# Pairs of heads put two to a step for the y and the p.v products, and 64 columns of ones in the sums over features

## The chip, the cores and the metric

The kernel runs on one core of a Trainium2 chip. The metric is the device time of one execution in microseconds (us); the median of three runs before the change is 1227.45 us (1226.97 to 1230.41). The core has five engines that run side by side: TensorE (PE in the rows, its weight loads PEld), VectorE (DVE), ScalarE (ACT), GpSimd (POOL), and SyncE (SP), which issues the loads. Matrix products are written to PSUM banks and taken out of them by VectorE and ScalarE.

## The reference

Two layers, each a mixer and a feed-forward net, on 256 tokens of 1024 features in float32. The mixer runs sparse attention and a state-space scan side by side; the lines below are those that the change touches.

```python
for l in range(DEPTH):                                   # DEPTH = 2
    h = rms_norm(x, norm1_g[l]) * (1.0 + sc1) + sh1
    proj = h @ w_in[l]                                   # 1024 x 10856
    ...
    s = jnp.einsum("bqhd,bqkhd->bhqk", qb, kg) * scale   # 16 heads of 64
    p = jax.nn.softmax(s, axis=-1)
    o = jnp.einsum("bhqk,bqkhd->bqhd", p, vg)            # the p.v products
    o_attn = o @ w_attn_o[l]
    ...
    cb = jnp.einsum("bclgn,bcsgn->bgcls", cm_c, bm_c)    # 4 groups of 8 heads
    y_diag = jnp.einsum("bgcls,bgrcls,bcsgrp->bclgrp", cb, decay, xs_c)   # the y products
    y = rms_norm((y + xs * d_skip) * silu(z), by group)  # a sum of squares over features
    o_ssm = y @ w_ssm_o[l]
    mixed = (sigmoid(ga) * o_attn + sigmoid(gm) * o_ssm) @ w_out[l]
    x = x + g1 * mixed
    h = rms_norm(x, norm2_g[l]) * (1.0 + sc2) + sh2      # a sum of squares over features
    u = causal_dwconv(h @ w_up[l])
    x = x + g2 * ((silu(gate) * val) @ w_down[l])
```

## The kernel before

Everything is kept with features on the partitions and the 256 tokens along the free dimension. Each float32 weight and activation is split into a high and a low part that TensorE takes at one pass (ScalarE copies the high part, `wh` for weights; VectorE subtracts it, `wl`), and each product of 128 x 128 weights with 256 tokens is three instructions: hi.hi, hi.lo, lo.hi. These are the main products, 8112 of them (`bk<-h,wh`, `bk<-u,wl` and the like), run by `run_fm` and `run_tm` in one fixed order, the chunks of `plan`. After every 12 of them (one output tile of a unit of 4 weight tiles) comes a call of `pump()`, which may let one step of side work into TensorE's program.

Side work is written as generators. `attention` (line 1582) and `ssd` (line 1688) stand in the queue `calm`, of which only the first is advanced, one step in a call. A step ends with `yield Need(...)`: the next one is let in when the tiles named are due by the kernel's own reckoning of time, and when as many of the four small PSUM banks as `banks=` says are free. So the place of each step among the main products follows from a planner's reckoning (`on_pe`, `after`, `plan_ahead`), and so does the order of instructions on VectorE, ScalarE and GpSimd, where each waiting piece has a priority (`urgent` raises it).

Two heads make a pair. For each of 8 pairs in a layer, `attention` does scores and softmax in step n, six transposes in step n+2 (`pT`), and the p.v products in step n+3 (lines 1626 to 1640): four float32 products with 64-column weights, 256 and 128 tokens wide for either head, then `hi_lo` of the result. For each of 16 pairs in a layer, `ssd` makes the decay in step n (a product with `sel`, ScalarE's `Exp`, VectorE's product with `cbm`) and the y products in step n+2 (lines 1719 to 1731): again four products with 64-column weights, then one VectorE instruction that adds `x_[i]` times `dsk`. A float32 product is two instructions in the trace, so one block of a pair is eight.

`token_sum` (line 1196) sums squares over features: two float32 products in which a 128 x 128 tile of squares is the weights and 16 columns of `ones` are moved; `inv_rms` reads one column of each.

```python
# lines 1201 and 1215
mm(st["ps"][:, 16 * t:16 * t + 16], sq[:, t * P:t * P + P], ones[:, 0:16], ...)
total = st["ps"][:, 0:32].rearrange("p (t c) -> p t c", c=16)[:, :, 0]
```

The adaLN weights of later layers are summed on VectorE in the gaps (`adacc`) and folded by TensorE (`bk<-adacc,ones`, weights of 32 columns). All instructions are issued by one helper, so every row of the profile has line 209, and rows are told apart by tile names: `p` is the shared tile of `pe`, `pT` and the decay `e`; `u` holds v, x, z and the split parts.

Of the kernel before, what the change touches and what calls it, by code (L numbers as in the profile page):

```python
# [15 lines left out]
ALU = mybir.AluOpType  # L16
# [3 lines left out]
P = 128  # L20
# [26 lines left out]
def trunk(ctx, tc, x, c, positions, w_ada, b_ada, norm1_g, w_in, q_norm_g, k_norm_g, ssm_conv_w, ssm_conv_b,  # L47
# [197 lines left out]
    def done(*tiles):  # L245
        for t in tiles:
            held.discard(t.tensor.name)
# [240 lines left out]
    def bank(pool=None):  # L488
        cnt[0] += 1
        pool = pool or sm  # L490
        t = pool.tile([P, 512], F32, tag="bank", name=f"bk{cnt[0]}")
        if pool is sm:
            bank_tag[0] = t.tensor.tag
        return t

    def mm(o, lhsT, rhs, start, stop):
        return T.matmul(o, lhsT, rhs, start=start, stop=stop, skip_group_check=True)
# [698 lines left out]
    def token_sum(st, total, sq):  # L1196
        def task():
            if st["ps"] is None:
                st["ps"] = bank()
            for t in range(2):  # L1200
                mm(st["ps"][:, 16 * t:16 * t + 16], sq[:, t * P:t * P + P], ones[:, 0:16],
                   st["n"] == 0 and t == 0, st["n"] == total - 1)
            st["n"] += 1
            if st["n"] == total and "then" in st:
                st["then"]()
            yield

        first_of_all.append(later(Need(sq, banks=0 if st["n"] else 1), task()))

    def inv_rms(st, scale, eps):  # L1210

        v = w_tile("rv", [P, 2])
        total = st.get("sum")
        if total is None:
            total = st["ps"][:, 0:32].rearrange("p (t c) -> p t c", c=16)[:, :, 0]
        st["rv"] = V.tensor_scalar(v, total, scale, eps, op0=ALU.mult, op1=ALU.add)
        r = w_tile("rr2", [P, 2])
        G.tensor_tensor(r, v, mhalf, op=ALU.pow)
        return r
# [117 lines left out]
    def mixer(l, link, link_out):  # L1337
# [244 lines left out]
        def attention(heads):  # L1582
# [4 lines left out]
            for n in range(len(pairs) + TD + PD):  # L1587
                if n < len(pairs):
# [20 lines left out]
                    with urgent():  # L1609
                        V.reciprocal(sums, sums)  # L1610
                        for j in range(2):
                            for t, cs in HALF:
                                G.tensor_scalar(pe[:, j, cs], pe[:, j, cs], sums[:, j, t:t + 1], 0.0, op0=ALU.mult, op1=ALU.add)
                if n - TD in pes:
                    pe = pes.pop(n - TD)
                    yield Need(pe, banks=2)
                    pT = pTs[n - TD] = hold(w_tile("pT", [P, 2, 384]))
                    pts = [bank(), bank()]
                    for j in range(2):
                        for b in range(3):  # L1620
                            T.transpose(pts[j][:, b * P:b * P + P], pe[:, j, b * P:b * P + P], ident)
                    done(pe)
                    with urgent():
                        for j in range(2):
                            A.activation(pT[:, j], pts[j][:, 0:384], AF.Copy)
                if n - TD - PD in pTs:
                    pT = pTs.pop(n - TD - PD)
                    i = pairs[n - TD - PD]
                    yield Need(pT, *vt[0][i // 4], *vt[1][i // 4], banks=1)
                    po = bank()  # L1630
                    for t, cs, src in ((0, slice(0, S), slice(0, S)), (1, slice(P, S), slice(S, 384))):
                        for j in range(2):
                            hh = 2 * i + j
                            vs = slice((hh % 4) * 64, (hh % 4) * 64 + 64)
                            mm(po[64 * j:64 * j + 64, cs], vt[t][hh // 8][(hh % 8) // 4][:, vs], pT[:, j, src], t == 0, t == 1)
                    done(pT)
                    if i % 2 == 1:
                        done(*(vt[t][i // 4][(i % 4) // 2] for t in range(2)))
                    with urgent():
                        hi_lo(po[:, 0:S], oT, i)  # L1640


        def ev_conv(base, dst, then=None):
# [44 lines left out]
        def ssd(g):  # L1688
# [12 lines left out]
            for n in range(4 + 2):  # L1701
                if n < 4:
# [13 lines left out]
                    yield Need(e, on="dve")  # L1716
                    with urgent():
                        V.tensor_tensor(e, e, cbm[g][:, None, :].to_broadcast([P, 2, 384]), op=ALU.mult)
                if n >= 2:
                    i = n - 2  # L1720
                    e = es.pop(i)
                    yield Need(e, cbm[g], *xdt, banks=1)
                    py = bank()
                    for cs, x, src in ((slice(0, S), xdt[0], slice(0, S)), (slice(P, S), xdt[1], slice(S, 384))):
                        for j in range(2):
                            hs = slice((2 * i + j) * 64, (2 * i + j) * 64 + 64)
                            mm(py[64 * j:64 * j + 64, cs], x[:, hs], e[:, j, src], x is xdt[0], x is xdt[1])
                    done(e)
                    m = 4 * g + i
                    with urgent():  # L1730
                        V.scalar_tensor_tensor(x_[i], x_[i], dsk[:, l, m:m + 1], py[:, 0:S], op0=ALU.mult, op1=ALU.add)
            while None in z_:
                yield
            warm.append(ssd_norm(g))
# [203 lines left out]
```

## Time and profile before

| | us |
|---|---|
| median of 3 runs | 1227.45 |
| lowest, highest | 1226.97, 1230.41 |
| the profiled execution | 1227.39 |
| its span from first to last instruction | 1225.7 |
| TensorE busy in it | 1201.3 (98%) |
| VectorE busy | 991.4 (81%) |
| ScalarE busy | 775.3 (63%) |
| GpSimd busy | 494.1 (40%) |

A matmul's row has a modelled end: it is told as 0.28 us long where the next one starts 0.11 to 0.12 us later. So a busy TensorE is read by the steps from start to start, and a row's idle time is 0.17 us less than what a wait costs.

### The profile page before, as it was taken

The page shows a single profiled execution, that of the slowest core. Times are in us where ns is not written, and L with a number is a line of the kernel's source. Part 1 is how long each engine was busy: PE and PEld are TensorE (multiplying, and loading weights), DVE is VectorE, ACT ScalarE, POOL GpSimd, SP SyncE. Part 2 cuts the span into 40 slices and gives each one's busy share as a digit, 9 for nine tenths or more (in the row PEclk, how much of TensorE's full clock was granted, in tenths as well). Part 3 has the DMA queues.
Part 4 walks back from the last instruction along what each step waited for, and adds up shares of the span by engine and source line. Part 5 has one row for each costly group of instructions (what it writes and reads, how often), then busy time and mean ns, then how long its engine had stood idle before and what let it go on. Part 6 is the DMA issues. An engine that isn't in the chain of part 4 may idle for free.

```text
span 1225.7 us, 24837 instructions
## 1 busy us (share of the span) xinstructions
PE 1201.3 (98%) x9835; PEld 1118.9 (91%) x9835; DVE 991.4 (81%) x1549; ACT 775.3 (63%) x1397; POOL 494.1 (40%) x503
## 2 busy tenths in 40 slices
PE   8999999999999999999999999999999999999998
PEld 7777898899988999999998778899999999999998
DVE  5488998778988789989767899888778757988863
ACT  4365577767865468778535557878578535877742
POOL 2163442216445225766202356314605313457710
PEclk9999999999999999999999999999999999999999
DMA  9765656655557666777665566264664665667551
GB/s 307 241 208 178 200 180 212 207 193 195 190 181 241 232 198 198 240 240 260 206 229 186 204 206 199 87 215 134 216 218 156 211 220 189 190 198 232 179 205 64
DMA packets 158665, 246.55 MB, mean 201 GB/s; under 512 B 11868, under 2 KB 66870, under 8 KB 158549
## 3 DMA queue, kind: packets, MB, share of 16 engines
q1 hardware_dynamic: 157989, 244.77, 60.1%
q8 instruction: 77, 1.26, 0.4%
q14 instruction: 39, 0.32, 0.1%
q0 software_dynamic: 288, 0.19, 0.1%
q10 hardware_dynamic: 272, 0.00, 0.0%
HBM read 243.89 MB, written 1.05 MB: 200 GB/s over the span
## 4 chain that ended last, share of the span: by engine, by line
PE 81%; DVE 12%; ACT 2%; issue 2%; POOL 1%; DMA 1%; SPq 0%; DVEq 0%; POOLq 0%; ACTq 0%
PE bk L209 81%; DVE wl L209 5%; DVE w L209 2%; DVE adacc L209 1%; ACT wh L209 1%; DVE p L209 1%; DVE u L209 1%; DVE t L209 1%; ACT w L209 1%; POOL rr L209 0%; DMA ad<-in_w_ada_dram 0%; POOL rows L209 0%; DVE top L209 0%; DVE mx L209 0%; POOL w L209 0%
## 5 line engine op out<-in xcount | busy, mean ns | idle before, releaser
L209 PE MATMUL bk<-h,wh 128*128 128x256 f32 x3296 | 588.1, 281 | 1.2 <-ACT h L209 1.1
L209 PEld LDWEIGHTS bk<-h,wh 128*128 128x128 f32 x3296 | 500.9, 189 | 12.0 <-issue 8.2
L209 DVE TENSOR_TENSOR wl<-st,wh 128x2048 fp32r<-128x2048 f32 (+1 forms) x200 | 439.8, 2206 | 67.3 <-ACT wh L209 67.0
L209 PE MATMUL bk<-h,wl 128*128 128x256 f32 x1648 | 457.9, 278 | 1.7 <-DVE wl L209 1.7
L209 ACT ACTIVATE wh<-st 128x2048 fp32r<-128x2048 f32 (+1 forms) x200 | 352.8, 1770 | 154.8 <-PE bk L209 129.9
L209 POOL TENSOR_TENSOR w<-w,w 128x254 f32<-128x254 f32 (+2 forms) x213 | 254.9, 1209 | 252.7 <-DVE w L209 173.4
L209 PEld LDWEIGHTS bk<-h,wl 128*128 128x128 f32 x1648 | 309.9, 188 | 2.4 <-DVE wl L209 1.9
L209 PE MATMUL bk<-u,wh 128*128 128x256 f32 x1312 | 232.6, 280 | 0.0
L209 PEld LDWEIGHTS bk<-u,wh 128*128 128x128 f32 x1312 | 199.3, 189 | 2.4 <-issue 2.4
L209 PE MATMUL bk<-u,wl 128*128 128x256 f32 x656 | 182.7, 278 | 0.6 <-DVE wl L209 0.6
L209 PE MATMUL bk<-wh,h 128*128 128x512 f32 x448 | 145.9, 402 | 3.1 <-DVE t L209 2.0
L209 ACT ACTIVATE w<-bk,vec 128x256 f32<-128x256 f32 (+2 forms) x256 | 119.7, 519 | 37.5 <-DVE w L209 26.0
L209 PEld LDWEIGHTS bk<-u,wl 128*128 128x128 f32 x656 | 123.2, 188 | 0.8 <-DVE wl L209 0.8
L209 DVE SCALAR_TENSOR_TENSOR adacc<-ad,chalf,adacc 128x512 f32<-128x512 f32 x140 | 119.0, 850 | 0.5
L209 PEld LDWEIGHTS bk<-wh,h 128*128 128x128 f32 x448 | 81.5, 188 | 23.9 <-issue 3.7
L209 POOL TENSOR_TENSOR u<-u,u 128x256 f32<-128x256 f32 (+1 forms) x56 | 74.1, 1348 | 63.1 <-DVE u L209 37.3
L209 PE MATMUL bk<-wl,h 128*128 128x512 f32 x224 | 88.7, 396 | 2.8 <-DVE wl L209 2.7
L209 DVE SCALAR_TENSOR_TENSOR w<-bk,vec,w 128x255 f32<-128x255 f32 (+1 forms) x176 | 80.3, 476 | 13.4 <-ACT w L209 11.9
L209 POOL TENSOR_TENSOR rr<-ss,mhalf 128x16 f32<-128x16 f32 x8 | 35.6, 4454 | 77.7 <-DVE ss L209 77.7
L209 POOL TENSOR_SCALAR p<-p,sums 128x128 f32<-128x128 f32 x64 | 35.6, 574 | 55.5 <-DVE sums L209 47.8
L209 ACT ACTIVATE u<-bk 128x128 f32<-128x128 f32 (+2 forms) x128 | 32.1, 321 | 39.8 <-PE bk L209 39.2
L209 PEld LDWEIGHTS bk<-wl,h 128*128 128x128 f32 x224 | 42.1, 188 | 13.4 <-DVE wl L209 4.6
(225 smaller groups left out, 1399.6 us busy)
## 6 DMA issues: line engine op xcount, KB each, us to landing
st<-in_w_in_dram SPq DMA_DIRECT2D x80, 1024.0 KB, 5.1
st<-in_w_up_dram SPq DMA_DIRECT2D x88, 512.0 KB, 5.2
ad<-in_w_ada_dram SPq DMA_DIRECT2D x160, 256.0 KB, 5.4
st<-in_w_down_dram SPq DMA_DIRECT2D x20, 1024.0 KB, 5.0
st<-in_w_ssm_o_dram SPq DMA_DIRECT2D x16, 1024.0 KB, 5.0
st<-in_w_ada_dram SPq DMA_DIRECT2D x16, 512.0 KB, 9.6
st<-in_w_attn_o_dram SPq DMA_DIRECT2D x8, 1024.0 KB, 5.1
st<-in_w_out_dram SPq DMA_DIRECT2D x8, 1024.0 KB, 5.1
```

The lines of the kernel that those rows point to most:

```text
L209: w.issue()
```

## The change

In `token_sum` and `inv_rms` the 16 columns of ones become 64, and the column read is the first of each 64. In `ssd` the y products are no longer done for one pair in each of the steps n = 2 to 5: those of pairs 0 and 1 are done together in step 3, those of 2 and 3 in step 5, behind one `Need` that names both decays and two banks. In `attention` the p.v products of two pairs are done together in every second step, now ahead of the transposes of that step.

```diff
-                mm(st["ps"][:, 16 * t:16 * t + 16], sq[:, t * P:t * P + P], ones[:, 0:16],
+                mm(st["ps"][:, 64 * t:64 * t + 64], sq[:, t * P:t * P + P], ones[:, 0:64],
...
-            total = st["ps"][:, 0:32].rearrange("p (t c) -> p t c", c=16)[:, :, 0]
+            total = st["ps"][:, 0:P].rearrange("p (t c) -> p t c", c=64)[:, :, 0]
...
+                if (n - TD - PD) % 2 == 1 and n - TD - PD in pTs:
+                    two = [(pTs.pop(k), pairs[k]) for k in (n - TD - PD - 1, n - TD - PD)]
+                    yield Need(*(t for pT, i in two for t in (pT, *vt[0][i // 4], *vt[1][i // 4])), banks=2)
+                    for pT, i in two:
+                        po = bank()
...
                 if n - TD in pes:
...
-                if n - TD - PD in pTs:
-                    pT = pTs.pop(n - TD - PD)
-                    i = pairs[n - TD - PD]
-                    yield Need(pT, *vt[0][i // 4], *vt[1][i // 4], banks=1)
-                    po = bank()
...
-                if n >= 2:
-                    i = n - 2
-                    e = es.pop(i)
-                    yield Need(e, cbm[g], *xdt, banks=1)
-                    py = bank()
...
+                if n in (3, 5):
+                    two = [(i, es.pop(i)) for i in (n - 3, n - 2)]
+                    yield Need(*(e for _, e in two), cbm[g], *xdt, banks=2)
+                    for i, e in two:
+                        py = bank()
```

The instructions stay the same in number on every engine; their order changes from the first attention of layer 0 on. On TensorE, the end of the first attention of layer 0, before; `p` is `pT`, `u` is v, the rows with `wh` and `wl` are main products:

```order
L209 MATMUL bk_2287<-h_727,wl_2203 128x256
L209 MATMUL bk_2534<-p_397_2463,u_1085 64x256 x2
L209 MATMUL bk_2534<-p_397_2463,u_1087 64x128 x2
L209 MATMUL bk_2537<-h_297,wh_2289 128x256
L209 MATMUL bk_2537<-h_298,wh_2289 128x256
```

and now:

```order
L209 MATMUL bk_2287<-h_727,wl_2203 128x256
L209 MATMUL bk_2515<-p_382_2425,u_1085 64x256 x2
L209 MATMUL bk_2515<-p_382_2425,u_1087 64x128 x2
L209 MATMUL bk_2518<-p_395_2455,u_1085 64x256 x2
L209 MATMUL bk_2518<-p_395_2455,u_1087 64x128 x2
L209 MATMUL bk_2521<-h_297,wh_2289 128x256
L209 MATMUL bk_2521<-h_298,wh_2289 128x256
```

The block of the pair before, which stood 12 main products earlier, now stands directly ahead of this one.

On VectorE, in the scan of group 2 of layer 0, up to the split of the weights that main product 1706 is the first to use (`wl_4134`); `adacc` is the adaLN sum, `dsk` rows take y products out of a bank, `w` and `u<-w` rows are the convolution, before:

```order
L209 SCALAR_TENSOR_TENSOR adacc_3854<-ad_4001,chalf,adacc_3854 128x512
L209 TENSOR_TENSOR p_650_4197<-p_650_4197,cbm_348_2159 128x768
L209 SCALAR_TENSOR_TENSOR u_4060<-w_628_4059,w_626_4057 128x256
L209 SCALAR_TENSOR_TENSOR w_640_4109<-bk_3925,vec_293,w_640_4109 128x255
L209 SCALAR_TENSOR_TENSOR w_640_4109<-bk_3925,vec_293,w_640_4109 128x254
L209 SCALAR_TENSOR_TENSOR adacc_3854<-ad_4052,chalf,adacc_3854 128x512
L209 SCALAR_TENSOR_TENSOR u_3673<-u_3673,dsk,bk_4284 128x256
L209 SCALAR_TENSOR_TENSOR u_4108<-w_638_4107,w_636_4105 128x256
L209 SCALAR_TENSOR_TENSOR u_4112<-w_642_4111,w_640_4109 128x256
L209 TENSOR_TENSOR wl_4134<-st_3831,wh_4133 128x2048
L209 SCALAR_TENSOR_TENSOR u_3725<-u_3725,dsk,bk_4314 128x256
```

and now, up to the split of the same weights (`wl_4138`):

```order
L209 SCALAR_TENSOR_TENSOR u_4112<-w_638_4111,w_636_4109 128x256
L209 SCALAR_TENSOR_TENSOR w_640_4113<-bk_3938,vec_293,w_640_4113 128x254
L209 SCALAR_TENSOR_TENSOR u_3738<-u_3738,dsk,bk_4251 128x256
L209 SCALAR_TENSOR_TENSOR adacc_3995<-ad_4020,chalf,adacc_3995 128x512
L209 SCALAR_TENSOR_TENSOR u_3742<-u_3742,dsk,bk_4252 128x256
L209 SCALAR_TENSOR_TENSOR adacc_3995<-ad_4037,chalf,adacc_3995 128x512
L209 SCALAR_TENSOR_TENSOR u_4116<-w_642_4115,w_640_4113 128x256
L209 TENSOR_TENSOR wl_4138<-st_3844,wh_4137 128x2048
L209 TENSOR_TENSOR xdt_661_4294<-bk_4334,dth_869 128x512
```

Between the split before this one (main product 1658) and this one there stood 22 instructions: 3 of `p<-p,cbm`, 5 of `adacc`, 8 of `w`, 4 of `u<-w`, 2 of `dsk`. Now there are 21: 2, 3, 8, 4 and 4; all four y products of the group have been taken out ahead of the split.

On ScalarE, at the end of the state-space output product of layer 0, before (`h` is the high part of the merged features that the product with `w_out` reads, `wh` the high part of its later weights):

```order
L209 ACTIVATE h_5240<-u_4643 128x256
L209 ACTIVATE wh_5302<-st_5101 128x2048
L209 ACTIVATE h_5242<-u_4644 128x256
L209 ACTIVATE h_5281<-u_4694 128x256
L209 ACTIVATE h_5283<-u_4695 128x256
```

and now:

```order
L209 ACTIVATE h_5225<-u_4663 128x256
L209 ACTIVATE h_5227<-u_4664 128x256
L209 ACTIVATE h_5258<-u_4702 128x256
L209 ACTIVATE wh_5346<-st_5150 128x2048
L209 ACTIVATE h_5260<-u_4703 128x256
```

A split of weights now stands between the third and the last `h` of layer 0; in layer 1 it is the other way round: it stood there before, and now follows the last `h`.

## Rows read from the trace of the kernel before

**Rows 1.** The page, part 1: busy us of each engine, share, instructions.
```profile
PE 1201.3 (98%) x9835; PEld 1118.9 (91%) x9835; DVE 991.4 (81%) x1549; ACT 775.3 (63%) x1397; POOL 494.1 (40%) x503
```

**Rows 2.** The page, part 4: the chain that ended last, by engine.
```profile
PE 81%; DVE 12%; ACT 2%; issue 2%; POOL 1%; DMA 1%; SPq 0%; DVEq 0%; POOLq 0%; ACTq 0%
```

**Rows 3.** Groups by form on PE: shapes, count | busy us, mean ns | idle before.
```profile
L209 PE MATMUL bk<-h,wh 128*128 128x256 f32 x3296 | 588.1, 281 | 1.2 <-ACT h L209 1.1
...
L209 PE MATMUL bk<-p,xdt 128*64 128x256 f32 x128 | 21.3, 413 | 0.0
...
L209 PE MATMUL bk<-ones,w 128*128 128x16 f32 x92 | 11.6, 246 | 0.0
L209 PE MATMUL bk<-p,u 128*64 128x256 f32 x64 | 10.6, 404 | 0.0
```

**Rows 4.** Timeline on PE around one y block: start us, us, instruction, xcount.
```profile
260.46 0.39 PE L209 MATMUL bk<-u,wh 128*128 128x256 f32 x2
260.69 0.28 PE L209 MATMUL bk<-u,wl 128*128 128x256 f32 x1
260.89 0.87 PE L209 MATMUL bk<-p,xdt 128*64 128x256 f32 x8
261.70 0.38 PE L209 MATMUL bk<-u,wh 128*128 128x256 f32 x1
```

**Rows 5.** Timeline on PE where two blocks already stand together, layer 1.
```profile
767.53 0.76 PE L209 MATMUL bk<-uext,adt 128*64 128x256 f32 x3
768.02 0.43 PE L209 MATMUL bk<-p,u 128*64 128x256 f32 x1
...
768.23 0.81 PE L209 MATMUL bk<-p,u 128*64 128x256 f32 x7
768.98 0.50 PE L209 MATMUL bk<-h,wh 128*128 128x256 f32 x2
```

**Rows 6.** Waits of PE from 196 to 1220 us: total us, times, longest.
```profile
PE bk L209 <- DVE wl L209: 3.5, 3, 1.7
PE bk L209 <- ACT xdt L209: 1.2, 1, 1.2
PE bk L209 <- ACT h L209: 1.1, 1, 1.1
PE bk L209 <- DVE adacc L209: 0.9, 1, 0.9
```

**Rows 7.** Timeline on PE around one sum with 16 columns of ones.
```profile
443.29 0.52 PE L209 MATMUL bk<-ones,w 128*128 128x16 f32 x4
443.65 0.48 PE L209 MATMUL bk<-h,wh 128*128 128x256 f32 x2
```

**Rows 8.** Timeline on PE around two float32 products that move 128 columns.
```profile
451.97 0.61 PE L209 MATMUL bk<-ident,rr 128*128 128x128 f32 x4
452.33 0.48 PE L209 MATMUL bk<-p,wh 128*128 128x258 f32 x2
```

**Rows 9.** Timeline on PE at three of these waits: [idle before <-what ended it].
```profile
343.43 0.39 PE L209 MATMUL bk<-h,wl 128*128 128x256 f32 x1 [1.74 <-DVE wl L209]
...
396.06 0.85 PE L209 MATMUL bk<-xdt,wh 128*128 128x256 f32 x2 [1.22 <-ACT xdt L209]
...
611.81 0.38 PE L209 MATMUL bk<-u,wl 128*128 128x256 f32 x1 [0.63 <-DVE wl L209]
```

**Rows 10.** Stretch of 3.4 us: busy of PE, PEld, DVE, ACT, POOL, PEclk, DMA share, GB/s.
```profile
344.60:348.00 3.40, 3.40 (x18) 2.47 (x17) 2.87 (x5) 0.42 (x1) 3.32 (x3) 0.50 0.97 334
```

**Rows 11.** Timeline on DVE ahead of the first of these waits.
```profile
325.04 1.50 DVE L209 TENSOR_TENSOR p<-p,cbm 128x768 f32<-128x768 f32 x1
326.46 2.36 DVE L209 SCALAR_TENSOR_TENSOR adacc<-ad,chalf,adacc 128x512 f32<-128x512 f32 x2
...
330.17 0.47 DVE L209 SCALAR_TENSOR_TENSOR u<-u,dsk,bk 128x256 f32<-128x256 f32 x1
...
340.56 2.81 DVE L209 TENSOR_TENSOR wl<-st,wh 128x2048 fp32r<-128x2048 f32 x1
```

More of the change, by code (lines that the diff above doesn't have):

```diff
@@ L1613, in attention @@
                                 G.tensor_scalar(pe[:, j, cs], pe[:, j, cs], sums[:, j, t:t + 1], 0.0, op0=ALU.mult, op1=ALU.add)
+                if (n - TD - PD) % 2 == 1 and n - TD - PD in pTs:
[3 more added lines that the diff above has]
+                        po = bank()
+                        for t, cs, src in ((0, slice(0, S), slice(0, S)), (1, slice(P, S), slice(S, 384))):
+                            for j in range(2):
+                                hh = 2 * i + j
+                                vs = slice((hh % 4) * 64, (hh % 4) * 64 + 64)
+                                mm(po[64 * j:64 * j + 64, cs], vt[t][hh // 8][(hh % 8) // 4][:, vs], pT[:, j, src], t == 0, t == 1)
+                        done(pT)
+                        if i % 2 == 1:
+                            done(*(vt[t][i // 4][(i % 4) // 2] for t in range(2)))
+                        with urgent():
+                            hi_lo(po[:, 0:S], oT, i)
                 if n - TD in pes:
@@ L1625, in attention @@
                             A.activation(pT[:, j], pts[j][:, 0:384], AF.Copy)
-                if n - TD - PD in pTs:
-                    pT = pTs.pop(n - TD - PD)
-                    i = pairs[n - TD - PD]
-                    yield Need(pT, *vt[0][i // 4], *vt[1][i // 4], banks=1)
-                    po = bank()
[L1631 to L1640, printed above, removed]
         def ev_conv(base, dst, then=None):
@@ L1718, in ssd @@
                         V.tensor_tensor(e, e, cbm[g][:, None, :].to_broadcast([P, 2, 384]), op=ALU.mult)
-                if n >= 2:
-                    i = n - 2
-                    e = es.pop(i)
-                    yield Need(e, cbm[g], *xdt, banks=1)
-                    py = bank()
[L1724 to L1731, printed above, removed]
+                if n in (3, 5):
[3 more added lines that the diff above has]
+                        py = bank()
+                        for cs, x, src in ((slice(0, S), xdt[0], slice(0, S)), (slice(P, S), xdt[1], slice(S, 384))):
+                            for j in range(2):
+                                hs = slice((2 * i + j) * 64, (2 * i + j) * 64 + 64)
+                                mm(py[64 * j:64 * j + 64, cs], x[:, hs], e[:, j, src], x is xdt[0], x is xdt[1])
+                        done(e)
+                        m = 4 * g + i
+                        with urgent():
+                            V.scalar_tensor_tensor(x_[i], x_[i], dsk[:, l, m:m + 1], py[:, 0:S], op0=ALU.mult, op1=ALU.add)
             while None in z_:
```

## The prediction

> **What bounds the kernel now.** I read the page first. TensorE is busy for 98% of the span [rows 1] and makes up 81% of the chain that ended last, with VectorE second at 12% [rows 2]: an engine that hardly ever stands still can be made faster only by taking time out of its own stream, or by removing the few waits that are left. The groups by form show the stream: thousands of main products, and beside them the y and p.v blocks, which alone (with one small product) use weights of 64 columns [rows 3]. The timeline then gives what a block costs, from start to start, since the modelled ends overlap [rows 4, 5]. Last come TensorE's waits: after 196 us, where the order begins to change, they are few, and four kinds make up nearly all, 3.5 + 1.2 + 1.1 + 0.9 = 6.7 us [rows 6]. No load is among them.
>
> The profiled execution took 1227.39 us, the median is 1227.45: the same, so I sum against 1227.4.
>
> **The change part by part.**
>
> *The pairing, on TensorE.* Main products start 0.115 us apart (0.23 us for two, from 260.46 to 260.69). The block at 260.89 starts 0.20 us after the main product ahead of it, so 0.09 us goes into changing over to 64-column weights; from its start to the next main product pass 0.81 us [rows 4]. One block alone thus costs 0.09 + 0.81 = 0.90 us, two cost 1.80. The trace has one place where two blocks of the same widths already stand together: from 767.53 to 768.98, 1.45 us for both [rows 5]. With one entry, 0.09, that is 1.54 us. A pair of blocks saves 0.26 us. There are 128 / 4 = 32 y and 64 / 4 = 16 p.v blocks [rows 3], and in the new order all 48 stand two by two, so 24 x 0.26 = 6.2 us. Blocks that stood behind a fold of `adacc` shared a change-over; there were two such places and now there is one, which gives back 0.09. I take **6.1 us**. Bounds: at the least only the second entry is saved, 24 x 0.09 = 2.2 us, if the second block paid its exit again. At the most it is what the shared visit shows [rows 5], since there the second block already costs only 1.45 - 0.81 = 0.64 us; I take this end, because that row has the same widths and the same kind of weights (its first block used only half of the array's columns, which leaves some doubt).
>
> *The ones.* Four instructions of 16 moved columns take 0.36 us until the next main product [rows 7]; four of 128 columns with weights of the same shape also take 0.36 us [rows 8]. 64 lies between, so 92 instructions [rows 3] cost nothing more: **0**, with both bounds at 0 to within 0.02 us each, 46 x 0.02 = 0.9 us either way. VectorE reads two numbers as before.
>
> [...]
>
> *The waits.* An idle time of a row is 0.17 us short of what it costs: a main product is drawn 0.28 us long where the next starts after 0.115.
>
> At 343.43 TensorE had waited 1.74 us for a split of weights [rows 9], 1.91 us in all. Just behind it the granted clock was 0.50, the lower of its two levels (1.2 of 2.4 GHz), for 3.4 us [rows 10]; half of that, 1.7 us, was lost too. The split was late because 22 VectorE instructions stood between the split before and it, from 325.04 to 340.56, 15.5 us [rows 11]. In the new order there are 21: one `p<-p,cbm` fewer (1.42 us to the next start), two `adacc` fewer (1.2 each where the two stood together, 0.7 at the least, so 1.4 to 2.4), two `dsk` more (0.4 each): 2.0 to 3.0 us earlier. TensorE itself comes later by 0.3: between main products 1658 and 1706 it did two single blocks, 1.80, and now does one pair, 1.54, and eight transposes, about 0.6. So 1.91 - 2.0 - 0.3 is below zero: wait and slow clock go, **3.6 us**. This is the term I trust least; if the wait only shrinks below 1 us, the 1.7 us of slow clock probably go with it.
>
> At 396.06 the state-space output product waited 1.22 us for the last normalised features of group 3 [rows 9], 1.4 us. The product that spreads this group's norm stood at main product 2016, and now at 1968, because `ssd` ends in fewer steps; the use stays at 2049. 48 products of 0.115 are 5.5 us more room: **1.4 us** go. In layer 1 it moves the other way, from 5988 to 6036, with the use at 6105: 69 products, 7.9 us, where the chain in layer 0 took some 5.6 us. No new wait there.
>
> At 611.81 a split was 0.63 us late [rows 9]. In the new order it stands ahead of two updates of `xt`, of the subtractions behind them and of one `adacc`, over 3 us of work: **0.8 us** go.
>
> The wait for `h`, 1.1 us in layer 1 [rows 6], came from a split that stood ahead of the last `h` on ScalarE. That split now follows it in layer 1, and the same split stands ahead of it in layer 0: **0**, it changes its layer. The third wait for `wl`, 3.5 - 1.74 - 0.63 = 1.1 us, has the same order around it and stays. The folds of `adacc` (0.9) come some 70 to 130 main products later; I leave their wait as it is.
>
> *New waits.* A pair's step waits for the later of two decays and for two of four small banks. TensorE runs in order, so behind its first product the 12 main products of the next tile would be queued, and VectorE's `dsk` rows, or `hi_lo` on ScalarE and VectorE, wait for them. All 48 blocks of before went in without such a wait [rows 6], and the new steps are let in by the same reckoning. Two results now leave the banks back to back, 0.4 us more of VectorE ahead of whatever follows. The orders of VectorE, of ScalarE, of GpSimd and of SP's loads all shift; what hides the loads is that none of TensorE's waits here was for one [rows 6]. For the unseen I allow **1.5 us**, one wait of the size seen here (0.6 to 1.9), with 0 and 8 us as ends (none; all the 6.7 us of before come back elsewhere, with a little of the slow clock).
>
> Sum: 1227.4 - 6.1 - 3.6 - 1.4 - 0.8 + 1.5 = **1217.0 us**.
>
> **The rivals.**
>
> *The waits only change place.* VectorE is busy for 81% [rows 1] and was late at 343 after 15.5 us without rest [rows 11]; if it is late elsewhere by as much, only TensorE's saving is left: 1227.4 - 6.1 = 1221.3. For it: every order on four engines changes, and before had luck of its own. Against: the named waits have named causes that the order removes.
>
> *VectorE takes the saving.* Where it, not TensorE, sets the pace, a faster TensorE only waits sooner. Then about 1227.4 - 2 = 1225.5, or no change at all. Against: the waits on VectorE are 4.4 us of 1020 [rows 6].
>
> *The pairing makes splits late (slower).* Two evictions in a row, and a burst of decays ahead of them, push the split of weights behind. If at most of the 24 pairs TensorE waited 0.6 us, that is 14 us: 1217.0 + 14 = 1231. It decides from the point where a split is done less than about 0.5 us ahead of its use; at 343 that was so, elsewhere in the scans it was not, or there would be more waits [rows 6]. Two or three waits as that at 343, with the slow clock behind each (3.6 us), do the same.
>
> *The pairing doesn't do what it says.* If the second block pays entry and exit again, the saving is between 0 and 2.2 us: 1217.0 + 3.9 to 6.1, or 1221 to 1223. The shared visit speaks against it [rows 5].
>
> *Wider sums cost their columns.* At the pace of the main products, 0.115 us for 256 columns, 48 columns are 0.02 us, twice for each float32 pass at most: 92 x 0.02 to 0.04 = 2 to 4 us, 1219 to 1221. [...] The rows at either width speak against it [rows 7, 8].
>
> **How the numbers follow.** Forecast, 1213.5 to 1219.5: 0.50. Waits change place, or one of the two small rivals on TensorE, 1219.5 to 1223.7: 0.26. Better still (no new wait, and the waits for `adacc` gone), below 1213.5: 0.07. VectorE takes the saving, 1223.7 to 1231.1: 0.10. Slower: 0.07. A difference of 0.3%, 3.7 us, is about what can be told from no change, so faster is below 1223.7: 0.83, same 0.10, slower 0.07. The range 1212 to 1224 holds the forecast, the second case, and most of the better one: about 0.8.
>
> **What would show it.** TensorE's timeline: 24 visits of two blocks, about 1.54 us from the main product ahead to the one behind beyond its own step; if each takes near 1.8, the first term is wrong. Four instructions of 64 columns until the next main product: 0.36 us, or the second is wrong. The waits of TensorE: no long one for `wl` in the scans of layer 0 and no stretch at clock 0.50 behind it; none for `xdt`; one of about 1 us for `h`, in layer 0; one of about 1 us for `wl` near 660 us. Waits for `p` at y blocks, or more than 6 us of waits in all after 196 us, would prove the forecast of the waits wrong.

## The result, and the profile after

The changed kernel takes **1215.1 us** (median of 4 runs, 1213.23 to 1219.64), the kernel before 1227.94 (4 runs, 1226.97 to 1230.41): a ratio of 0.9898, with a 95% interval of 0.9867 to 0.9929. The forecast was 1217.0, range 1212 to 1224. The profiled execution took 1215.03 us, so it is 12.4 us shorter than the profiled one of before.

The page shows how that came about in two lines: busy time of each engine, and the engines' shares of the chain that ended last. They answer to [rows 1, 2].

```profile
PE 1187.8 (98%) x9835; PEld 1112.9 (92%) x9835; DVE 994.6 (82%) x1549; ACT 774.3 (64%) x1397; POOL 478.5 (39%) x503
...
PE 72%; DVE 17%; ACT 5%; issue 2%; POOL 2%; DMA 1%; SPq 0%; DVEq 0%; ACTq 0%; POOLq 0%
```

TensorE has 13.5 us less work in as many instructions. VectorE and ScalarE have as much as before, and their shares of the chain rose, from 12% to 17% and from 2% to 5%: the end hangs on them more often.

**The visits.** TensorE's timeline around one pair of y blocks (start us, us, instruction, count) answers to [rows 4]:

```profile
284.82 0.28 PE L209 MATMUL bk<-h,wl 128*128 128x256 f32 x1
285.03 1.52 PE L209 MATMUL bk<-p,xdt 128*64 128x256 f32 x16
286.48 0.50 PE L209 MATMUL bk<-h,wh 128*128 128x256 f32 x2
```

From the main product ahead to the one behind pass 1.66 us; less the main product's own step of 0.115 that is 1.54, the price that the prediction gave. Of the other 23 visits 21 are within 0.01 us of it; one stands right behind a fold of `adacc`, one with the `uext` products, as it did before [rows 5]. Two single visits of before cost 2 x 0.90 (from 260.69 to 261.70, less a step) [rows 4].

A visit costs more than that, since the first step between the two main products behind it is late as well. In before, behind the block of [rows 4]:

```profile
261.70 0.50 PE L209 MATMUL bk<-u,wh 128*128 128x256 f32 x2
262.04 0.28 PE L209 MATMUL bk<-u,wl 128*128 128x256 f32 x1
```

Two steps take 0.34 us there, where two main steps usually take 0.23: the first is 0.22 us long. It is so behind single blocks and behind pairs (in the changed kernel from 286.48 to 286.82, 0.34). From main product 744 on, 47 visits of before have such a step, 5.1 us in all beyond the usual one, and the 24 of the changed kernel 2.7: another 2.4 us that the pairing saves.

**The sums.** Four instructions that move 64 columns, until the next main product:

```profile
437.39 0.55 PE L209 MATMUL bk<-ones,w 128*128 128x64 f32 x4
437.75 0.48 PE L209 MATMUL bk<-h,wh 128*128 128x256 f32 x2
```

0.36 us, as with 16 columns [rows 7].

**The waits.** TensorE's waits from 196 to 1220 us (sum, times, longest) answer to [rows 6]:

```profile
PE bk L209 <- DVE wl L209: 5.9, 6, 1.4
PE bk L209 <- ACT adarow L209: 1.0, 1, 1.0
PE bk L209 <- ACT h L209: 0.8, 1, 0.8
...
PE bk L209 <- DVE adacc L209: 0.3, 2, 0.2
```

The wait for `xdt` is gone and the one for `adacc` is small, but splits of weights are now late six times instead of three, and the longest of these waits is the old one, with 1.45 us instead of 1.74.

**Where the 12.4 us are.** Adding up TensorE's steps from start to start by the kind of work gives the table; where a step is booked is in part a choice, so a row is good to about half a us. The second row of it is no merit of the change: up to 192 us both kernels run the same work. What differs is TensorE's clock at the start. These are the same 18 products, before and after:

```profile
9.24 4.21 PE L209 MATMUL bk<-ones 128*128 128x128 f32 x18 [0.98 <-DVE xt L209]
```

```profile
9.24 2.27 PE L209 MATMUL bk<-ones 128*128 128x128 f32 x18 [0.70 <-DVE xt L209]
```

They start at the same time and take nearly twice as long before, close to the two to one of the clock's levels (2.4 and 1.2 GHz); the first stretch of full clock on record begins at 13.5 us before and at 8.3 us after. In the 14 traces of this study it begins between 7.7 and 15.6 us, and the first main product between 21.9 and 25.2.

| us | before | after | difference |
|---|---|---|---|
| whole execution | 1227.4 | 1215.0 | -12.4 |
| up to main product 744, where the orders part | 192.0 | 190.1 | -1.9 |
| y and p.v blocks | 43.2 | 38.0 | -5.2 |
| other small work, with the change from and to it | 79.8 | 77.3 | -2.6 |
| sums over features | 8.9 | 8.7 | -0.3 |
| main products beyond 113.5 ns each | 11.7 | 7.8 | -4.0 |
| waits | 9.3 | 10.8 | +1.5 |
| half of the time at clock 0.50 | 1.6 | 1.7 | 0.0 |

The blocks' row is less than 24 x 0.25 = 6.0, since a block that stands next to other small work shares its change-over with it, and the table puts that under the other work. The late first steps behind the visits are there too: they are the largest part of the 2.6 us of that row. The row on main products was in no forecast: they run at one of two steps, 113 to 114 or 117 to 118 ns, and fewer of them now run at the slow one (some 1300 instead of 2200 of those with 256 columns).

### The profile page after: what moved, and what is told of

It is laid out like the page before. It is cut to its first block, busy times and chain, and to the rows that moved or that the text cites. A ratio compares the mean times of both kernels' runs of the same rounds, so it can differ in the third digit from the quotient of the medians.

```text
span 1213.3 us, 24830 instructions
## 1 busy us (share of the span) xinstructions
PE 1187.8 (98%) x9835; PEld 1112.9 (92%) x9835; DVE 994.6 (82%) x1549; ACT 774.3 (64%) x1397; POOL 478.5 (39%) x503
## 4 chain that ended last, share of the span: by engine, by line
PE 72%; DVE 17%; ACT 5%; issue 2%; POOL 2%; DMA 1%; SPq 0%; DVEq 0%; ACTq 0%; POOLq 0%
PE bk L209 72%; DVE wl L209 7%; DVE w L209 3%; ACT wh L209 2%; ACT w L209 2%; DVE adacc L209 1%; DVE u L209 1%; DVE t L209 1%; DMA st<-in_w_in_dram 1%; ACT p L209 1%; DVE p L209 1%; POOL w L209 1%; POOL rr L209 1%; SPq L209 0%; DMA st<-in_w_ada_dram 0%
## 5 line engine op out<-in xcount | busy, mean ns | idle before, releaser
L209 POOL TENSOR_TENSOR w<-w,w 128x254 f32<-128x254 f32 (+2 forms) x213 | 244.9, 1162 | 218.6 <-DVE w L209 174.9
L209 POOL TENSOR_TENSOR u<-u,u 128x256 f32<-128x256 f32 (+1 forms) x56 | 66.5, 1211 | 96.5 <-DVE u L209 71.3
L209 POOL TENSOR_SCALAR p<-p,sums 128x128 f32<-128x128 f32 x64 | 42.0, 674 | 52.7 <-DVE sums L209 50.0
L209 PEld LDWEIGHTS bk<-wl,h 128*128 128x128 f32 x224 | 42.1, 188 | 13.5 <-DVE wl L209 4.6
```

What stands on the lines that cost most here:

```text
L209: w.issue()
```

## The experiments

**Each edit by itself.** Theory: the gain is 24 saved change-overs on TensorE; the wider sums are worth nothing. Rivals: the sums, or the order that the planner makes for them, carry part of it. *The pairing alone:*

```
-mm(st["ps"][:, 64 * t:64 * t + 64], sq[:, t * P:t * P + P], ones[:, 0:64],
+mm(st["ps"][:, 16 * t:16 * t + 16], sq[:, t * P:t * P + P], ones[:, 0:16],
...
```

> The changed kernel with its sums back at 16 moved columns: the pairing alone. Theory (the gain is the 24 saved change-overs to 64-column weights, 0.25 us each, and the wider sums are worth nothing): 24 visits of 1.66 us from the main product ahead to the one behind, four instructions of 16 columns in 0.48 us as at 64, and the time of the changed kernel, 1215, plus or minus 4 us for waits that fall differently, since the planner reckons a sum of 16 columns 24 ns longer per instruction and so orders the engines a little differently. Rival one (the wider sums, or the order that the planner makes for them, carry part of the gain): 1219 or more. Rival two (the wider sums cost their columns, 2 to 4 us): 1211 to 1213, with sums shorter than 0.46 us.

Measured: 1213.9 us, ratio 0.9881 (0.9863 to 0.9900), visits of 1.66 us, sums of 0.48 us from the main product ahead. Neither rival holds: the pairing alone is as good as the whole change.

*The sums alone*, the same lines changed the other way in the kernel before:

> The kernel before with its sums at 64 moved columns: the wider sums alone. Theory (they cost and give nothing on TensorE): 48 visits of one block at 1.01 us, sums of 0.48 us, and the time of the kernel before, 1227, plus or minus 4 us for waits that fall differently. Rival one (the order that the planner makes for the wider sums carries part of the gain): 1217 to 1222. Rival two (the columns cost): 1229 to 1231 with sums longer than 0.5 us.

Measured: 1239.4 us, ratio 1.0086 (1.0071 to 1.0101). It fell outside the theory and outside both rivals: 10 us slower, with sums of 0.48 us. The waits of TensorE tell why (same columns as above):

```profile
PE bk L209 <- DVE wl L209: 4.9, 4, 1.7
PE bk L209 <- DVE u L209: 1.6, 1, 1.6
...
PE bk L209 <- POOL p L209: 0.9, 1, 0.9
PE bk L209 <- ACT p L209: 0.8, 1, 0.8
```

Against [rows 6] there are new waits for `u`, `p` and more for `wl`, some 5.5 us in all; main products lose 2.9 us more at their slow step, and other small work takes 1.2 us more. (The profiled execution, 1240.6 us, also had two stretches at clock 0.50 ahead of 90 us, where the work is that of before; two of the four runs, 1238.3 us, show a higher mean clock.) The planner reckons 119.5 ns for an instruction of 64 columns and 143 for one of 16, so its clock moves, and with it the order on every engine. To separate the columns from the order, the next kernel moves 64 columns and lets the planner go on reckoning with 16:

```
+if n == 64 and rhs.tensor.name == ones.tensor.name:
+    n = 16
 kind = "r" if rhs.dtype == F32R ...
...
```

> The kernel before with its sums at 64 moved columns, while the planner still reckons them as 16, so that the order on every engine stays that of the kernel before. The kernel with the wider sums alone had taken 1239, 10 us more than before, with sums as short as at 16 columns in its trace. Theory (the columns cost nothing; the 10 us are waits of another order): sums of 0.48 us and 1227 to 1229.5, as the kernel before, with its waits at the same places (1.7 us near 344, 1.2 near 396, 1.1 near 1019). Rival (the wider sums themselves cost, by their columns or by the clock that falls behind them): 1235 or more.

Measured: 1228.5 us, ratio 0.9996 (0.9986 to 1.0005), with the waits of before where they were:

```profile
PE bk L209 <- DVE wl L209: 3.8, 3, 1.7
PE bk L209 <- ACT xdt L209: 1.2, 1, 1.2
PE bk L209 <- ACT h L209: 1.1, 1, 1.1
```

So the columns cost nothing, and the 10 us were the order's. A last run on this takes the changed kernel and widens the sums to 128 columns, which the planner reckons as 223 ns:

```
-mm(st["ps"][:, 64 * t:64 * t + 64], sq[:, t * P:t * P + P], ones[:, 0:64],
+mm(st["ps"][:, P * t:P * t + P], sq[:, t * P:t * P + P], ones,
...
```

> The changed kernel with its sums at 128 moved columns. Theory (columns cost nothing up to 128 under weights of 128 columns; what moves the time is the order, since the planner now reckons a sum 104 ns longer per instruction): sums of 0.48 us as at 16 and 64, and a time that differs from 1215 only by waits, up to 10 us either way as the kernel with the wider sums alone showed; the work on TensorE without waits within 1 us of the changed kernel's. Rival (columns cost at the pace of the main products, 0.115 us for 256, that is 0.03 us for 64 more in each instruction, perhaps twice): sums of 0.6 us or more and 3 to 5 us more of TensorE's work.

Measured: 1221.0 us, ratio 0.9938 (0.9922 to 0.9954), again with sums as short as ever:

```profile
299.22 0.60 PE L209 MATMUL bk<-ones,w 128*128 128x128 f32 x4
299.58 0.48 PE L209 MATMUL bk<-h,wh 128*128 128x256 f32 x2
```

0.36 us for 16, 64 and 128 columns, 90 ns an instruction. The Trainium skill (page "TensorE: Matmul & The Clock Gate", section "Back-to-back issue gap") has a gap that grows with the columns moved for a single product by itself, and says that in a stream of weight loads and products both set the spacing, so that for few columns this gap counts too little. The trace agrees: here the time does not follow the columns. Behind main product 744 this kernel's trace has 5.7 us over the changed kernel's: main products at the slow step take 4.9 us more and the waits 1.2, and the rest takes a little less.

**The price of the change-over.** Two kernels keep the changed kernel's order on every engine and add the same 24 instructions, one 128-column transposition for each pair, issued with the last product of a block and unknown to the planner; in one kernel it stands between the two blocks, in the other behind them:

```
 def issue():
     r = nc.tensor.matmul(o, lhsT, rhs, ...)
+    if extra is not None:
+        nc.tensor.transpose(extra, ident, ident)
     return r
```

> The changed kernel with one 128-column transposition of the identity (0.11 us) put between the two blocks of each of the 24 pairs, unseen by the planner, so that the order on every engine stays that of the changed kernel. Theory (what a pair saves is one change to 64-column weights and back): each visit is longer by 0.11 + 0.25 us, 2.0 us instead of 1.66, 24 x 0.36 = 8.7 us in all; waits on VectorE shrink by about 1 us, since TensorE reaches the weights later; about 1223. Rival (the saving comes from fewer steps and evictions side by side, not from the change of width): only the transposition is paid, 24 x 0.11 = 2.7 us, about 1218.

> The changed kernel with the same transposition put behind the second block of each of the 24 pairs, order kept. In the traces of before and after the main products run at one of two steps, 113 to 114 or 117 to 118 ns, and keep it until other work comes; behind a 64-column block the slow step is the usual one, behind transpositions of 128 columns the fast one. Theory (the work just ahead sets the step): the runs of main products behind the 24 visits are all fast, which gives back 1.0 us of the 1.24 us that they lose in the changed kernel; the transpositions cost 24 x 0.11 = 2.7 us; about 1217, and 6 us less than with the transposition between the blocks. Rival (the step has another cause, or is chance): as many slow runs behind the visits as in the changed kernel, 16 of 24; about 1218.

Measured: 1224.2 us between (ratio 0.9962, 0.9949 to 0.9975), 1216.5 behind (0.9907, 0.9886 to 0.9927). TensorE's timeline (in these kernels the helper stands in line 498, the transposition in line 506), between the blocks:

```profile
263.97 0.87 PE L498 MATMUL bk<-p,xdt 128*64 128x256 f32 x8
264.77 0.33 PE L506 MATMUL bk<-ident 128*128 128x128 f32 x1
265.03 0.87 PE L498 MATMUL bk<-p,xdt 128*64 128x256 f32 x8
265.83 0.50 PE L498 MATMUL bk<-u,wh 128*128 128x256 f32 x2
```

and behind them:

```profile
261.01 0.28 PE L498 MATMUL bk<-u,wl 128*128 128x256 f32 x1
261.21 1.52 PE L498 MATMUL bk<-p,xdt 128*64 128x256 f32 x16
262.66 0.33 PE L506 MATMUL bk<-ident 128*128 128x128 f32 x1
262.75 0.48 PE L498 MATMUL bk<-u,wh 128*128 128x256 f32 x2
```

2.07 us against 1.74 for the same instructions: 0.33 x 24 = 7.8 us, and the medians differ by 7.6. Behind a visit the transposition costs 0.09 us until the next main product. If it costs that between the blocks as well, a change to 64-column weights and back is worth 0.32 us; if it costs there what an ordinary product in the last experiment did, 0.17, it is worth 0.25, the term of the prediction. Either way the rival, 1218 for the kernel with the transposition between, is out: the saving comes from the change of width, with no change of order. The late first step behind a visit has no part in this price, since it comes once in either kernel.

**More blocks in a visit.** If each merged visit saves 0.25 us, four y blocks at a time should save 2 us more. The first attempt let two blocks share a bank:

```
-if n in (3, 5):
-    two = [(i, es.pop(i)) for i in (n - 3, n - 2)]
+if n == 5:
+    two = [(i, es.pop(i)) for i in range(4)]
...
-        py = bank()
+        if i % 2 == 0:
+            pys = bank()
+        py = pys[:, i % 2 * S:i % 2 * S + S]
...
-                mm(..., x is xdt[0], x is xdt[1])
+                mm(..., x is xdt[0] and i % 2 == 0, x is xdt[1])
```

> The changed kernel with all four y blocks of a group in one visit: 8 visits of four blocks in place of 16 of two (two blocks share a bank, so the step asks for two banks as before). Theory (each visit costs one change of width, each further block 0.65 us): a visit of four takes 0.11 + 0.89 + 3 x 0.65 = 2.95 us from the main product ahead to the one behind, against 2 x 1.66 for two visits of two with one main step more between them, so each saves 0.25 us, 2.0 us in all: 1213, plus or minus 4 for waits that fall differently (the first two decays of a group are held longer, and four results leave the banks back to back). Rival (four evictions in a row make VectorE late with the splits): new waits of 1 us or more behind several of the 8 visits, 1219 or more.

The same with sums of 16 columns:

> The same visits of four, with the sums at 16 columns. Theory: 2.0 us less than the pairing alone, which had 1213.9, so 1212, plus or minus 4 for the waits; visits of 2.95 us. Together with the run before it this is a second order for the same work on TensorE, so the difference between the two tells what the order alone is worth. Rival (four evictions in a row make VectorE late): 1218 or more.

Measured: 1244.2 us (ratio 1.0128, 1.0097 to 1.0159) and 1235.7 (1.0066, 1.0049 to 1.0082), the slowest way of grouping. One of the visits on TensorE's timeline, with the idle time before an instruction and what ended it in brackets:

```profile
369.84 0.87 PE L209 MATMUL bk<-p,xdt 128*64 128x256 f32 x8
372.25 1.52 PE L209 MATMUL bk<-p,xdt 128*64 128x256 f32 x16 [1.54 <-DVE u L209]
375.32 0.87 PE L209 MATMUL bk<-p,xdt 128*64 128x256 f32 x8 [1.55 <-DVE u L209]
```

TensorE stands behind the first and behind the third block: the second block of a bank waits until VectorE has read the first. The Trainium skill (page "PSUM — Partial Sum Buffer", section "PSUM bank collisions raise a hardware error") has two engines on the same partitions of one bank at once as an error. The program keeps them apart by a wait; the trace of the first of these two kernels shows its price, 15 waits with 18.2 us in sum, 1.2 each. My expectation had not seen that the shared bank is a wait. With a bank for each block (four small banks asked for, `py = bank()` for each):

> The changed kernel with all four y blocks of a group in one visit, each block in a bank of its own (the step asks for four banks). In the run where two of the four shared a bank, TensorE stood inside the visits, 15 waits of 1.2 us on average, for the result of the block ahead to leave the shared bank; the time without these waits was not seen. Theory (the shared bank made those waits): visits of 2.95 us without a wait inside, TensorE's work for y and p.v 2.0 us less than in the changed kernel, and 1213 plus or minus 4 for the order; if the order is an unlucky one, as with the wider sums alone, the loss is in waits at other places, not in the visits. Rival (four blocks at once are too many for VectorE and the banks): waits of 0.5 us or more inside or right behind most of the 8 visits, 1220 or more.

Measured: 1218.5 us, ratio 0.9917 (0.9894 to 0.9941). The visits are as reckoned:

```profile
358.72 0.28 PE L209 MATMUL bk<-h,wl 128*128 128x256 f32 x1
358.93 2.82 PE L209 MATMUL bk<-p,xdt 128*64 128x256 f32 x32
361.68 0.50 PE L209 MATMUL bk<-h,wh 128*128 128x256 f32 x2
```

2.96 us without a wait inside, in all eight, and the y and p.v rows are 1.6 us less than in the changed kernel. Yet the kernel is no faster. Its waits are 2 us more, among them these, which the changed kernel does not have, and main products lose 2.3 us more at the slow step:

```profile
PE bk L209 <- ACT xdt L209: 1.2, 1, 1.2
PE bk L209 <- DVE adt L209: 1.2, 1, 1.2
```

The shared bank is thereby shown as the cause of the waits inside the visits; waits and slow steps of another order take back what the 1.6 us less work had brought.

**The wait that should have gone.** The prediction let the wait at 343 us and the slow clock behind it go. In the changed kernel two adacc folds stand ahead of the late split; this kernel leaves them out and keeps the order:

```
 step = V.scalar_tensor_tensor(acc, st, chalf[:, k:k + 1], acc, ...)
+if i in (43, 44):
+    step.issue = lambda: None
```

> The changed kernel with two of VectorE's adacc folds left out, the two that stand ahead of the late split of weights near 334 us (part of the second layer-0 modulation sum is therefore missing from the output); the order is otherwise kept. They take 1.03 + 0.75 = 1.8 us from start to start. Theory (at 338 VectorE's own work is what TensorE waits for): the wait of 1.45 us there is gone or under 0.1 us, the rest of the trace is as in the changed kernel, and the time is 1.6 us less, 1213 to 1214. Rival (the split waits for its other input from ScalarE, or for a load, and the folds only fill that time): the wait stays at 1 us or more and the time at 1215.

Measured: 1215.9 us, ratio 0.9899 (0.9874 to 0.9924). At the place, TensorE's timeline has no wait left, though it reaches the weights at the same point of its order:

```profile
338.98 0.38 PE L209 MATMUL bk<-h,wl 128*128 128x256 f32 x1
```

The theory holds there: VectorE's own work is what TensorE waited for, and 1.6 us are gained from main product 1700 to 1710. The whole time does not show them, so that part of the expectation fell. The two profiled executions took the same 1215.03 us. In this one the opening took 2.1 us longer (its first full clock on record is at 14.0 us, the changed kernel's at 8.3), the stretch at clock 0.50 near 421 us, worth 1.7, did not come, and between 580 and 810 us about 1.4 us were lost again, 0.45 of them in a wait at a p.v block that was not there before; the rest of this loss is not traced to a place. Whether the two folds are worth 1.6 us of the whole is thus not shown.

The other way to be rid of waits for weights is to let the planner put every split first:

```
-V.tensor_tensor(lo[:, k:k + step], ...)
+with urgent(URGENT if now[0] > 180000.0 else 0):
+    V.tensor_tensor(lo[:, k:k + step], ...)
```

> The changed kernel with VectorE's half of each split of weights entered as urgent work behind 180 us, so that the planner puts it ahead of folds, updates and evictions. Theory one (TensorE's waits for wl, 5.9 us in six of them, come from where the planner puts the splits): they are gone or under 0.5 us each, nothing else is late, and the time is 1208 to 1211. Theory two (VectorE has too little room there, so a wait that is taken away in one place comes up in another): the waits for wl shrink, but waits for what now stands behind the splits (u, p, xdt, h, adacc) take their place, 4 us or more in sum, and the time is 1213 to 1222.

Measured: 1229.6 us, ratio 1.0009 (0.9994 to 1.0023): as slow as before the change, worse than either theory. The waits from 196 to 1220 us:

```profile
PE bk L209 <- DVE t L209: 3.7, 2, 2.8
PE bk L209 <- DVE w L209: 2.2, 1, 2.2
PE bk L209 <- DVE h L209: 2.0, 1, 2.0
PE bk L209 <- DVE wl L209: 1.2, 1, 1.2
```

The waits for `wl` fell from 5.9 to 1.2 us and 8 us of waits for three other results of VectorE took their place; besides, the granted clock was 0.50 twice for 3.4 us. That is theory two, at a higher price than I gave it.

**What sets the step of the main products.** The transposition behind a visit gave 20 fast runs of main products out of 24; in the changed kernel 8 of 24 were fast. Two runs of main products behind a visit, nine steps each, in the changed kernel and with the transposition:

```profile
286.82 0.28 PE L209 MATMUL bk<-h,wl 128*128 128x256 f32 x1
...
287.88 0.28 PE L209 MATMUL bk<-h,wl 128*128 128x256 f32 x1
```

```profile
287.50 0.28 PE L498 MATMUL bk<-h,wl 128*128 128x256 f32 x1
...
288.53 0.28 PE L498 MATMUL bk<-h,wl 128*128 128x256 f32 x1
```

1.06 / 9 = 118 ns and 1.03 / 9 = 114 ns. Is it the transposition, or any full-width instruction? The last kernel puts an ordinary product there, `matmul(extra, ones, ones)`, in place of the transposition:

> The changed kernel with one ordinary product (ones by ones, 128 weights and 128 moved columns, of the same kind as the main products) put behind the second block of each of the 24 pairs, order kept. With a transposition in that place 20 of the 24 runs of main products behind a visit went at the fast step, 113 to 114 ns, against 8 of 24 in the changed kernel. Theory (a run behind the 64-column blocks is slow because main products follow them directly, and a transposition resets the step while a product of the main kind does not): at least 14 of the 24 runs are slow, and the time is that of the changed kernel plus 24 products at 0.1 us, about 1217.5. Rival (any full-width instruction in between resets the step): 18 or more of 24 fast, 1 us less, 1216.5.

Measured: 1217.5 us, ratio 0.9919 (0.9894 to 0.9944), and 23 of the 24 runs fast. My theory falls and the rival holds: one full-width instruction between the 64-column blocks and the main products is enough. It does not pay: until the next main product it costs 0.17 us, the transposition 0.09, and the first step behind either is shorter than behind a block, 0.17 and 0.21 us against 0.22 to 0.23; but a visit's run loses only 0.05 us at the slow step (1.24 us over 24).

## Why the prediction was right, and where it was not

*The pairing, -6.1: right in kind, too small.* The visits take 1.54 us, as the shared visit [rows 5] had said, and a change-over with the order kept is worth 0.25 to 0.32 us. The upper bound was the right end to take. But I read the price only as far as the first main product behind a block. The late step behind that one, 0.11 us a visit, goes with each visit that disappears, which makes 2.4 us more.

*The ones, 0: right on TensorE, and incomplete.* The 92 instructions cost nothing. (Their bounds counted 46 groups; 92 instructions are 23 groups of four, so 0.02 us each is 0.5 us and not 0.9.) But I costed the edit only there. Its width is also a number that the planner reckons with; alone it made the kernel before 10 us slower, which is more than any term of my sum. Together with the pairing it happens to cost nothing that can be told (1215.1 against 1213.9).

*The wait at 343 and its slow clock, -3.6: wrong, the step that failed.* Of three numbers two were right. The rows are VectorE's half of the earlier split and its first use on TensorE in before, and then both splits and both uses in after:

```profile
322.84 2.28 DVE L209 TENSOR_TENSOR wl<-st,wh 128x2048 fp32r<-128x2048 f32 x1
...
334.04 0.28 PE L209 MATMUL bk<-h,wl 128*128 128x256 f32 x1
```

```profile
320.19 2.29 DVE L209 TENSOR_TENSOR wl<-st,wh 128x2048 fp32r<-128x2048 f32 x1 [0.85 <-ACT wh L209]
...
335.58 2.82 DVE L209 TENSOR_TENSOR wl<-st,wh 128x2048 fp32r<-128x2048 f32 x1
```

```profile
329.13 0.28 PE L209 MATMUL bk<-h,wl 128*128 128x256 f32 x1
...
338.46 0.39 PE L209 MATMUL bk<-h,wl 128*128 128x256 f32 x1 [1.45 <-DVE wl L209]
```

From the end of one split to the end of the next VectorE took 18.2 us before (to 343.37, [rows 11]) and takes 15.9: 2.3 less, inside the 2.0 to 3.0 that I gave. From one use to the next, the wait left out, TensorE took 7.65 us before (to 341.69) and takes 7.88: 0.2 more, where I said 0.3. Together 2.6 us are gained. The third number I never wrote down: how long the earlier split had been done when TensorE came for it. It was 8.9 us before and is 6.65 now, so 2.3 of the 2.6 us were gone before the stretch began, and the wait shrank by 0.29 us.

Why the room is smaller, the brackets tell: VectorE stood idle ahead of the earlier split, for ScalarE's half of it. These are ScalarE's rows there, before and after:

```profile
320.48 1.92 ACT L209 ACTIVATE wh<-st 128x2048 fp32r<-128x2048 f32 x1 [0.38 <-PE bk L209]
```

```profile
316.11 1.36 ACT L209 ACTIVATE p<-bk,acs 128x256 f32<-128x256 f32 x4 [0.82 <-PE bk L209]
...
318.26 1.90 ACT L209 ACTIVATE wh<-st 128x2048 fp32r<-128x2048 f32 x1
```

Before, ScalarE began this half 13.6 us ahead of the use (334.04), and the next decay came behind it; now a decay of 2.2 us (316.11 to 318.26) stands ahead, and 10.9 us are left. That this room belongs to the order, and not to a TensorE that has become faster, a run shows: with the transposition between the blocks TensorE reaches these weights 5.3 us later, and the three splits ahead of this stretch are done 4.09, 4.47 and 5.64 us before their use, against 4.08, 4.46 and 5.63 in the changed kernel. (The split at issue is done 7.06 us before its use there, against 6.65: one visit, longer by 0.41, lies between.) I had compared the order of VectorE between two splits, and not that of ScalarE ahead of the first.

The slow clock did leave that place, but fell elsewhere: from 421.35 to 424.75 the granted clock was 0.50 (columns as in [rows 10]).

```profile
421.35:424.75 3.40, 3.40 (x18) 3.40 (x17) 2.02 (x5) 0.56 (x3) 0.00 (x0) 0.50 0.96 295
```

It begins 1.5 us after the end of the wait for `h` (419.81). In the four other traces with this order the same wait, 0.78 to 0.79 us, was followed by the full clock, so this stretch belongs to the execution and not to the kernel. At the old place the wait, now 1.45 us, was followed by the full clock.

*The other waits: right one by one, wrong in sum.* The waits for `xdt` at 396 and for the split at 611 are gone, the one for `h` stands in layer 0, the one near 668 is at 660 with 1.2 us, and no y or p.v block waits. For new waits I allowed 1.5 us; there came late splits at 464 (0.4), 499 (0.9), 555 (1.0) and 1124 (0.9 us) and one wait for `adarow` at 1139 (1.0): 4.2 us, and the waits for `adacc` and the old one for `adarow` gave back 0.9. I had said that more than 6 us of waits behind 196 us would prove the forecast of the waits wrong; they are 8.0 without those for `xt` at the end. For the waits, the rival "the waits only change place" is what happened, and the run with urgent splits shows it at its plainest: what is put ahead of one wait stands behind another.

*The number.* With the waits as they came the sum is 1227.4 - 6.1 + 1.5 = 1222.8. The measured 1215.1 is below that for three reasons that were not in it: main products at the slow step (-4.0), the late first steps behind the visits (-2.4), and an opening that happened to be 1.9 us shorter in the profiled execution, by its clock. Together they make 1214.5; the half us that is left is within what the table can tell. So the forecast hit 1217.0 partly by errors that cancel. Of the 4.0 us, 1.5 belong to the visits (2.75 us lost behind 48 of them, 1.24 behind 24), a loss that one full-width instruction takes away; 2.5 are in long runs of main products behind the `adarow` transpositions, 4 to 5 us in two traces with the order of before, 1 to 3 in five with the order of after. Why these runs stay slow for a shorter time is open.

## What to carry to other kernels

Grouping instructions that use another width of weights saves one change-over for each visit that disappears, and most of its price can be read off any place where two already stand together; read on behind the next main product, since the step after it can be late as well. Before a wait is struck from the list, write down how long the last thing that was in time had been done, and look up in the new order, on every engine that makes it, whether that room is still there. Where a planner sets the order, the numbers that it reckons with are part of an edit; to learn what an instruction costs, change it with the order held, and to learn what an order is worth, change only the reckoning.

## What the runs showed of the hardware

- Main products of 128 weights and 256 columns run at one of two steps, 113 to 114 or 117 to 118 ns, and keep it for many products. Behind 64-column blocks it was the slow one in 16 of 24 runs (15 of 24 in two other kernels with the same order), behind float32 sums of 64 columns in 11 of 11, but of 128 columns in 4 of 10; one full-width transposition or product in between made 20 and 23 of 24 runs fast. What it is in the engine, no run shows.
- Behind the visits of 64-column blocks the first step between main products of 256 columns was 0.22 to 0.23 us, where 0.114 is usual; behind a transposition put there 0.20 to 0.21, behind an ordinary product 0.17.
- Four float32 instructions under 128 weights take 0.36 us until the next main product with 16, 64 or 128 columns moved.
- A second block in a bank waits for the first one's result to be read: 1.2 us each on average, nearly twice the 0.65 us that a further block costs.
- The granted clock fell behind a wait of 0.78 us in one of five traces with the same order, and stayed full behind one of 2.80 us (the kernel with urgent splits, at 729 us). At the start of the execution it was full from 7.7 us in one trace and only from 15.6 us in another.
